# DeltaNet key blocks: decay rows from one 512-column product of diagonals, norms from the diagonals of the key products, one beta scaling per head, both directions of the block inverse in one pass

## The chip, the cores and the metric

One core of a Trainium2 chip. The metric is device time in microseconds (us) of one execution. The engines are TensorE (PE), VectorE (DVE), ScalarE (ACT) and GpSimd (POOL); SyncE (SP) and POOL issue the transfers (DMA). In the profile PEld is TensorE's weight load, which overlaps PE.

## What the kernel computes

A two-layer trunk over 256 context tokens and 256 latent tokens of width 1024. Every layer is half-step SwiGLU, token mixer, half-step SwiGLU; the first mixer is a recurrent scan (RG-LRU), the second is a gated DeltaNet with 8 heads of width 128, in both directions, in chunks of 64 tokens. Only the DeltaNet matters here. For each head and chunk, cut from the reference:

```
k = l2norm(k);  g_cum = cumsum(g)
decay = exp(where(incl, g_cum[:, None] - g_cum[None, :], -inf))
a_mat = where(strict, (k * beta) @ k.T * decay, 0) + eye(64)
sol = triangular_solve(a_mat, concat([v * beta, k * beta * exp(g_cum)]))
qk = (q @ k.T) * decay
```

and then a scan over the chunks with a 128x128 state for each head and direction. There are 4 context and 4 latent chunks, so 8 in each direction.

## The kernel before, in words

Everything is held feature-major: a product has 128 features on the partitions and the tokens as columns. A weight tile is split into a high and a low part, and each 128x128 block of a projection is three products (lines 297 to 299, tile `f` in this stage). The stage `deltanet` (line 953) runs 32 projection tiles of 128 output features, in the order of `SEQ`: 8 of keys, 8 of queries (latent tokens only, 256 columns), then values (512 columns) and output gates (latent only) interleaved. Four key tiles go first, with the stage's norm; the loop at the end of `deltanet` runs the other 28. `project` calls `tick` after every second block of eight, which advances three groups of generators: the decays, the heads' own work (convolution of four taps, one on ACT at line 783 and three on DVE at line 787, then SiLU), and, from the tenth tile on, `keys`.

`keys` starts `k_rest` for one head every four ticks, up to three heads in step, then computes the norms, then runs `solve`, and when the projections of the values are through, `merge`. What stands on each engine in which order is not written out in this stage: the framework's planner orders every engine's instructions from the program order and its own costs. (In the other stages the order of some or all engines is the program's.)

`k_rest` (line 1065) does for one head:

1. ACT squares the keys (lines 1068 and 1048), 512 columns in two instructions.
2. TensorE builds `gr`, 128x512, the cumulated gates of each chunk as rows: for each of two directions and four chunk pairs one 64x64 transpose of a broadcast column (line 1076) and one 64x64 product with the identity (line 1077). A product in full 32-bit floats is two instructions on TensorE, a transpose is one: 24 in all.
3. TensorE forms the sums of the squares with a vector of ones (lines 1080 and 1083, 12 instructions), then the eight 64x64 products of keys with keys, `kk` (line 1087, 16 instructions).
4. DVE subtracts the column gates from `gr` into `e` (line 1091), ACT applies Relu and Exp (lines 1097 and 1098): `e` holds the decay factors. DVE adds the epsilon to the sums of squares (1094), takes the reciprocal (1100) and scales beta by it into `bp` (1102).
5. DVE takes the latent quarter of `e` into `QK` (1108) and multiplies `e` by `kk` (1110).
6. `e` is scaled by `bp` and laid out for the inverse: four 32-row diagonal blocks into `Bc` (line 1118, one on DVE, three on POOL), and four off-diagonal blocks into `MO` (line 1123, all on DVE). Each of the eight instructions does the scaling and the placing at once.

`solve` (line 1210) inverts the 32x32 blocks of all heads by 31 steps of elimination. A step is four DVE instructions: the outer product into `tm` for each direction (line 1223) and the subtraction for each direction (line 1227). Four 128x1024 transposes end it (lines 1230 and 1231). `merge` joins the 32-blocks to 64-blocks with small products on TensorE, and `scan` (line 1358) runs the chunks.

The value and gate weights were split in an earlier stage and kept in DRAM; POOL issues their loads (line 205) into a ring of eight tiles. A POOL load waits until TensorE has read the tile that it replaces. Working tiles of 128x512 come from a pool with five buffers (`phase(5)`).

Of the kernel before, what the change touches and what calls it, by code (L numbers as in the profile page):

```python
# [59 lines left out]
for _name, _w in (("U1", 128), ("L1", 128), ("U1s", 128), ("L1s", 128), ("U1f", 128), ("L1f", 128),  # L60
                  ("CH0", 1), ("CH1", 1), ("cap", 128), ("sel32", 32)):
    MSK[_name] = (_n, _n + _w)
    _n += _w
# [31 lines left out]
def trunk(ctx, tc, io):  # L95
# [853 lines left out]
    def deltanet(norm, next_norm, sp, hp, pools, done):  # L949
# [21 lines left out]
        KQ, QK, VN, Z, KT = ({} for _ in range(5))  # L971
# [5 lines left out]
        def sv(p):  # L977
            return pools[1].tile([128, 32, 32], F32, name=nm(p), tag="sv", bufs=3)
# [10 lines left out]
        def decays(w):  # L989
# [35 lines left out]
            DVE.tensor_copy(gc, q[:, 0:64])  # L1025
            ACT.activation(gt.rearrange("p c x -> p (c x)"), q[:, 192:320], AF.Exp)
# [38 lines left out]
        def k_rest(hd):  # L1065
            kq = KQ[hd]
            sq = slot("sq")
            ACT.activation(sq[:, 0:256], kq[:, 0:256], AF.Square)
            squares(sq[:, 256:512], kq, slice(0, 4, 3))
            yield from pause(PACE["k_lag"])  # L1070
            gr = bank("gr")
            for dr in range(2):
                for j in range(4):
                    o = slice(dr * 256 + j * 64, dr * 256 + j * 64 + 64)
                    c = dr * 32 + j * 8 + hd
                    PE.transpose(gr[LO, o], gc[LO, c:c + 1].to_broadcast([64, 64]), ident[LO, LO])
                    PE.matmul(gr[HI, o], gc[HI, c:c + 1].to_broadcast([64, 64]), ident[HI, HI], start=True, stop=True)
            kk = bank("kk")
            for j in range(2):
                PE.matmul(kk[:, 256 + j:257 + j], sq[:, j * 128:j * 128 + 128], ones, start=True, stop=True)  # L1080
            for i in range(4, 8):
                j = slot_of(i)
                PE.matmul(kk[ROWS[i % 2], 256 + j:257 + j], sq[:, i * 64:i * 64 + 64], ones, start=True, stop=True)
# [9 lines left out]
            rs = small("rs", 4)  # L1093
            DVE.tensor_scalar(rs, kk[:, 256:260], EPS, None, OP.add)
            ACT.copy(ss[:, :, hd], kk[:, 256:260])
            if True:
                ACT.activation(e, e, AF.Relu, scale=-1.0)
            ACT.activation(e, e, AF.Exp, scale=-1.0)
            yield
# [13 lines left out]
            yield  # L1113
            for b in range(4):
                r = slice(32 * b, 32 * b + 32)
                x = slice(32 * (b % 2), 32 * (b % 2) + 32)
                out = Bc[r].rearrange("p d i (s h) -> p d s h i", h=8)[:, :, :, hd]
                (DVE if b < PACE["block_split"] else POOL).tensor_tensor(
                    out, e4[r, :, :, x], dsh(bp)[r, :, :, hd:hd + 1].to_broadcast([32, 2, 4, 32]), OP.mult)
            for dr in range(2):  # L1120
                for c in range(2):
                    r = slice(64 * c + 32 * dr, 64 * c + 32 * dr + 32)
                    (DVE if dr < PACE["mo"] else POOL).tensor_tensor(MO[dr][r, hd::8, :], e4[r, dr, :, 32 * (1 - dr):32 * (1 - dr) + 32],
                                       dsh(bp)[r, dr, :, hd:hd + 1].to_broadcast([32, 4, 32]), OP.mult)
# [85 lines left out]
        def solve():  # L1210
            N, XI = [sv("N") for _ in range(2)], [Bc[:, dr] for dr in range(2)]
# [6 lines left out]
            for j in range(31):  # L1218
                n, m = j + 1, 31 - j
                tm = [pools[1].tile([128, 256], F32, name=nm("tm"), tag="tm", bufs=2)[:, :m * n]  # L1220
                      .rearrange("p (i c) -> p i c", c=n) for _ in range(2)]
                for dr in range(2):
                    DVE.tensor_tensor(tm[dr], N[dr][:, j + 1:, j:j + 1].to_broadcast([128, m, n]),
# [533 lines left out]
```

## Time and profile before

| | us |
|---|---|
| median of 3 runs | 1897.73 |
| lowest, highest | 1894.87, 1900.56 |
| the profiled execution | 1894.58 |
| its span | 1892.8 |
| PE busy in the span | 1827.7 (97%) |
| DVE busy in the span | 1316.6 (70%) |
| ACT busy in the span | 803.3 (42%) |
| POOL busy in the span | 89.5 (5%) |

The span is cut into 40 slices of 47.3 us on the profile's page. "PEclk" is the clock that TensorE was granted, as a share of the full 2.4 GHz; its other level is one half, 1.2 GHz. A busy PE is not PE at its peak: matmuls are pipelined, and a stretch of small products looks as busy as one of large ones.

### The profile page before, as it was taken

What the parts mean: (1) busy time and instruction counts of PE and PEld (TensorE: products, weight loads), DVE (VectorE), ACT (ScalarE), POOL (GpSimd) and SP (SyncE); (2) the same over time, 40 slices, a digit from 0 to 9 for tenths busy, and PEclk for the clock granted to TensorE, in tenths of its full rate; (3) what the DMA queues carried; (4) which work ended last, traced back from release to release, by engine and by line L of the source; (5) the groups of instructions that cost most, each with busy time, mean ns of one, the idle gap of its engine ahead of it and who ended that gap; (6) DMA issues with size and microseconds to landing.
All of it is one profiled execution on the core that took longest, in us unless ns stands there. A gap on an engine that the chain in (4) does not pass through costs nothing.

```text
span 1892.8 us, 29201 instructions
## 1 busy us (share of the span) xinstructions
PE 1827.7 (97%) x11078; PEld 1585.6 (84%) x11078; DVE 1316.6 (70%) x2772; ACT 803.3 (42%) x1651; POOL 89.5 (5%) x130
## 2 busy tenths in 40 slices
PE   5999999999999999999999999999999989889997
PEld 3788888898779888888898888888988886789997
DVE  8867766787888768667466555546756976975555
ACT  5522132247874432333333322323654333845453
POOL 4100000000000000000000000000012230100000
PEclk9999999999999999999999999999978989989999
DMA  8344654542323766566417765743232550035553
GB/s 338 134 158 164 222 175 154 171 159 79 100 82 131 243 236 210 193 226 239 133 56 245 231 213 191 240 146 115 72 101 90 174 157 1 2 122 176 191 178 104
DMA packets 98061, 300.54 MB, mean 159 GB/s; under 512 B 10880, under 2 KB 20352, under 8 KB 97792
## 3 DMA queue, kind: packets, MB, share of 16 engines
q1 hardware_dynamic: 92160, 277.69, 43.6%
q0 software_dynamic: 5760, 20.97, 3.6%
q8 instruction: 87, 1.43, 0.3%
q14 instruction: 54, 0.44, 0.1%
HBM read 276.61 MB, written 22.02 MB: 158 GB/s over the span
## 4 chain that ended last, share of the span: by engine, by line
PE 86%; DVE 6%; issue 4%; ACT 3%; DMA 1%; POOL 0%; SPq 0%; POOLq 0%; DVEq 0%; ACTq 0%
PE gu L298 14%; PE gu L299 14%; PE gu L297 14%; PE fo L297 4%; PE fo L299 4%; PE fo L298 4%; PE tl L297 4%; PE tl L298 4%; PE tl L299 4%; PE f L297 2%; PE f L298 2%; PE f L299 2%; PE p L1416 1%; PE p L1405 1%; DVE hl L501 1%
## 5 line engine op out<-in xcount | busy, mean ns | idle before, releaser
L161 ACT CAST wp<-wr 128x512 fp32r<-128x512 f32 (+1 forms) x689 | 382.8, 607 | 293.8 <-DMA wr<-in_ffn_out_dram 69.3
L162 DVE TENSOR_TENSOR wp<-wr,wp 128x512 fp32r<-128x512 f32 (+1 forms) x689 | 432.7, 674 | 99.7 <-ACT wp L161 95.8
L298 PE MATMUL gu<-hl,wp 128*128 128x512 f32 (+1 forms) x1312 | 479.7, 366 | 9.2 <-DVE hl L501 9.2
L297 PE MATMUL gu<-hh,wp 128*128 128x512 f32 (+1 forms) x1312 | 479.3, 365 | 0.1
L299 PE MATMUL gu<-hh,wp 128*128 128x512 f32 (+1 forms) x1312 | 478.8, 365 | 0.0
L298 PEld LDWEIGHTS gu<-hl,wp 128*128 128x128 f32 x1312 | 248.9, 190 | 50.2 <-DVE hl L501 11.3
L403 DVE SCALAR_TENSOR_TENSOR junk<-ar,cb 128x1024 bf16<-128x1024 f32 x224 | 273.7, 1222 | 22.5 <-DMA ar<-in_w_adaT_dram 18.5
L297 PEld LDWEIGHTS gu<-hh,wp 128*128 128x128 f32 x1312 | 248.9, 190 | 40.4 <-ACT hh L499 0.6
L299 PEld LDWEIGHTS gu<-hh,wp 128*128 128x128 f32 x1312 | 249.1, 190 | 38.8
L653 ACT ACTIVATE sg<-gu 128x512 f32<-128x512 f32 (+1 forms) x88 | 47.8, 543 | 373.0 <-PE gu L299 362.9
L655 DVE TENSOR_TENSOR hf<-sg,gu 128x512 f32<-128x512 f32 (+1 forms) x88 | 54.5, 619 | 184.9 <-PE gu L299 131.2
L297 PE MATMUL tl<-hidh,wp 128*128 128x256 f32 (+1 forms) x418 | 139.7, 334 | 0.0
L298 PE MATMUL tl<-hidl,wp 128*128 128x256 f32 (+1 forms) x418 | 139.3, 333 | 0.0
L299 PE MATMUL tl<-hidh,wp 128*128 128x256 f32 (+1 forms) x418 | 139.2, 333 | 0.0
L297 PE MATMUL fo<-hidh,wp 128*128 128x512 f32 (+1 forms) x352 | 127.6, 362 | 0.0
L298 PE MATMUL fo<-hidl,wp 128*128 128x512 f32 (+1 forms) x352 | 127.6, 362 | 0.0
L299 PE MATMUL fo<-hidh,wp 128*128 128x512 f32 (+1 forms) x352 | 127.6, 362 | 0.0
L297 PE MATMUL f<-H,wp 128*128 128x256 f32 x320 | 98.0, 306 | 1.4 <-ACT sq L1048 1.1
L299 PE MATMUL f<-H,wp 128*128 128x256 f32 x320 | 96.3, 301 | 0.0
L298 PE MATMUL f<-H,wp 128*128 128x256 f32 x320 | 96.2, 301 | 0.0
L298 PEld LDWEIGHTS tl<-hidl,wp 128*128 128x128 f32 x418 | 79.4, 190 | 7.9
L297 PEld LDWEIGHTS tl<-hidh,wp 128*128 128x128 f32 x418 | 79.4, 190 | 7.8
(327 smaller groups left out, 2891.6 us busy)
## 6 DMA issues: line engine op xcount, KB each, us to landing
wr<-in_ffn_in_dram SPq DMA_DIRECT2D x172, 512.0 KB, 4.6
ar<-in_w_adaT_dram SPq DMA_DIRECT2D x128, 512.0 KB, 3.6
wr<-in_ffn_out_dram SPq DMA_DIRECT2D x64, 512.0 KB, 4.9
kp<-wp SPq DMA_DIRECT2D x80, 256.0 KB, 7.2
wp<-kp POOLq DMA_DIRECT2D x40, 512.0 KB, 4.9
wr<-in_dn_in_dram SPq DMA_DIRECT2D x32, 512.0 KB, 3.8
wr<-in_ffn_out_dram SPq DMA_DIRECT2D x64, 192.0 KB, 3.6
wr<-in_lru_in_dram SPq DMA_DIRECT2D x16, 512.0 KB, 4.3
```

Of the source, the lines that this page charges most:

```text
L161: ACT.copy(dst.hi, src)
L162: DVE.tensor_tensor(dst.lo, src, dst.hi.bitcast(F32), OP.subtract)
L297: PE.matmul(out, w.hi, x.hi, start=start, stop=False)
L298: PE.matmul(out, w.hi, x.lo, start=False, stop=False)
L299: PE.matmul(out, w.lo, x.hi, start=False, stop=stop)
L403: DVE.scalar_tensor_tensor(junk, raw, 1.0, cb[:, v], OP.mult, OP.mult, accum_out=m[:, t % 8, v:v + 1])
L501: DVE.scalar_tensor_tensor(lo, t, sh, hi.bitcast(F32), OP.add, OP.subtract)
L653: ACT.activation(sg[:, cols], P[0][:, cols], AF.Silu)
L655: DVE.tensor_tensor(hf[:, cols], sg[:, cols], P[1][:, cols], OP.mult)
L1405: PE.matmul(p2[:, 0:128], Yp[a][:, j * 8 + hd, :], rr, start=True, stop=True)
L1416: PE.matmul(p3[dr][:, 0:128], KT[hd][r2[dr], j * 128:j * 128 + 128], vs[r2[dr]], start=True, stop=True)
```

## The change

- Decay rows. `spread` is new: POOL multiplies an identity mask (`eye`, 64 columns, the same in both halves of the partitions) by the broadcast gate columns of a head into `GD`, 128x512: eight diagonals. `gr` is then one product of a 128x128 block mask of ones (`blk`) with `GD`, 512 columns, in full 32-bit floats. The transposes and the identity products go. Head 0's `GD` is made when the decays are known, each other head's when the head before it starts `k_rest`.
- Norms. The squares on ACT and their 12 TensorE instructions go. DVE multiplies the first 256 columns of `kk` by `eye` and sums each 64 columns (`tensor_reduce`); the result goes to `ss`, which ACT copied before.
- Scaling. DVE multiplies all of `e` by `bp` in one 128x512 instruction. The four `Bc` blocks are then plain copies on POOL (`tensor_scalar` by 1.0 plus 0.0), the four `MO` blocks plain copies on ACT. `k_rest` has one more yield.
- Inverse. The two directions' `N` and `tm` lie in one tile each, and a step is two DVE instructions of twice the size.
- Room: 7 instead of 5 working tiles, 1 instead of 3 buffers of `sv` (the two `N` are one tile of their own), 192 more mask columns, and the buffer for the descriptors of POOL's transfers is set to 8192 bytes for each partition (16384 where nothing is given).

```diff
-            return pools[1].tile([128, 32, 32], F32, name=nm(p), tag="sv", bufs=3)
+            return pools[1].tile([128, 32, 32], F32, name=nm(p), tag="sv", bufs=1)
...
             DVE.tensor_copy(gc, q[:, 0:64])
+            spread(0)
...
         def k_rest(hd):
             kq = KQ[hd]
-            sq = slot("sq")
-            ACT.activation(sq[:, 0:256], kq[:, 0:256], AF.Square)
-            squares(sq[:, 256:512], kq, slice(0, 4, 3))
+            if hd < 7:
+                spread(hd + 1)
             yield from pause(PACE["k_lag"])
+
             gr = bank("gr")
-            for dr in range(2):
-                for j in range(4):
-                    o = slice(dr * 256 + j * 64, dr * 256 + j * 64 + 64)
-                    c = dr * 32 + j * 8 + hd
-                    PE.transpose(gr[LO, o], gc[LO, c:c + 1].to_broadcast([64, 64]), ident[LO, LO])
-                    PE.matmul(gr[HI, o], gc[HI, c:c + 1].to_broadcast([64, 64]), ident[HI, HI], start=True, stop=True)
+            PE.matmul(gr, K_["blk"], GD.pop(hd), start=True, stop=True)
             kk = bank("kk")
-            for j in range(2):
-                PE.matmul(kk[:, 256 + j:257 + j], sq[:, j * 128:j * 128 + 128], ones, start=True, stop=True)
-            for i in range(4, 8):
-                j = slot_of(i)
-                PE.matmul(kk[ROWS[i % 2], 256 + j:257 + j], sq[:, i * 64:i * 64 + 64], ones, start=True, stop=True)
...
-            rs = small("rs", 4)
-            DVE.tensor_scalar(rs, kk[:, 256:260], EPS, None, OP.add)
-            ACT.copy(ss[:, :, hd], kk[:, 256:260])
-            if True:
-                ACT.activation(e, e, AF.Relu, scale=-1.0)
+            ACT.activation(e, e, AF.Relu, scale=-1.0)
             ACT.activation(e, e, AF.Exp, scale=-1.0)
+
+            dg, rs = slot("dg"), small("rs", 4)
+            dv = dg[:, 0:256].rearrange("p (s x) -> p s x", s=4)
+            DVE.tensor_tensor(dv, kk[:, 0:256].rearrange("p (s x) -> p s x", s=4), eye[:, 0].to_broadcast([128, 4, 64]), OP.mult)
+            DVE.tensor_reduce(ss[:, :, hd], dv, mybir.AxisListType.X, OP.add)
+            DVE.tensor_scalar(rs, ss[:, :, hd], EPS, None, OP.add)
...
+            DVE.tensor_tensor(e4, e4, dsh(bp)[:, :, :, hd:hd + 1].to_broadcast([128, 2, 4, 64]), OP.mult)
+            yield
             for b in range(4):
...
-                (DVE if b < PACE["block_split"] else POOL).tensor_tensor(
-                    out, e4[r, :, :, x], dsh(bp)[r, :, :, hd:hd + 1].to_broadcast([32, 2, 4, 32]), OP.mult)
+                POOL.tensor_scalar(out, e4[r, :, :, x], 1.0, 0.0, OP.mult, OP.add)
             for dr in range(2):
                 for c in range(2):
                     r = slice(64 * c + 32 * dr, 64 * c + 32 * dr + 32)
-                    (DVE if dr < PACE["mo"] else POOL).tensor_tensor(MO[dr][r, hd::8, :], e4[r, dr, :, 32 * (1 - dr):32 * (1 - dr) + 32],
-                                       dsh(bp)[r, dr, :, hd:hd + 1].to_broadcast([32, 4, 32]), OP.mult)
+                    ACT.copy(MO[dr][r, hd::8, :], e4[r, dr, :, 32 * (1 - dr):32 * (1 - dr) + 32])
+
+        def spread(hd):
+            GD[hd] = slot("gd")
+            POOL.tensor_tensor(GD[hd].rearrange("p (d s x) -> p d s x", d=2, s=4), eye.to_broadcast([128, 2, 4, 64]),
+                               dsh(gc)[:, :, :, hd:hd + 1].to_broadcast([128, 2, 4, 64]), OP.mult)
...
-                tm = [pools[1].tile([128, 256], F32, name=nm("tm"), tag="tm", bufs=2)[:, :m * n]
-                      .rearrange("p (i c) -> p i c", c=n) for _ in range(2)]
-                for dr in range(2):
-                    DVE.tensor_tensor(tm[dr], N[dr][:, j + 1:, j:j + 1].to_broadcast([128, m, n]),
-                                      XI[dr][:, j:j + 1, :n].to_broadcast([128, m, n]), OP.mult)
-                for dr in range(2):
-                    x = XI[dr][:, j + 1:, :n]
-                    DVE.tensor_tensor(x, x, tm[dr], OP.subtract)
+                tm = pools[1].tile([128, 512], F32, name=nm("tm"), tag="tm", bufs=1)[:, :2 * m * n]
+                tm = tm.rearrange("p (d i c) -> p d i c", d=2, c=n)
+                DVE.tensor_tensor(tm, Nb[:, :, j + 1:, j:j + 1].to_broadcast([128, 2, m, n]),
+                                  Bc[:, :, j:j + 1, :n].to_broadcast([128, 2, m, n]), OP.mult)
+                x = Bc[:, :, j + 1:, :n]
+                DVE.tensor_tensor(x, x, tm, OP.subtract)
...
-    with tc.tile_pool(name="dns", bufs=1, reuse_waits="tile") as dns, phase(5):
+    with tc.tile_pool(name="dns", bufs=1, reuse_waits="tile") as dns, phase(7):
...
-    nc = bacc.Bacc("TRN2", target_bir_lowering=False, num_devices=1)
+    nc = bacc.Bacc("TRN2", target_bir_lowering=False, num_devices=1, dynamic_dma_scratch_size=8192)
```

## Rows read from the trace of the kernel before

**Rows 1.** Busy us by stretch: length, engines (instructions), clock, DMA share, GB/s.

```profile
1383.00:1472.00 89.00, 87.86 (x719) 75.76 (x720) 51.81 (x134) 39.56 (x86) 23.16 (x36) 0.79 0.31 97
1472.00:1539.00 67.00, 65.08 (x668) 63.90 (x667) 64.72 (x179) 22.03 (x64) 20.44 (x34) 0.97 0.65 196
```

**Rows 2.** The same of tile `gr` alone: PE, PEld, DVE, clock, DMA.

```profile
1383.00:1472.00 89.00, 28.71 (x192) 19.08 (x192) 5.53 (x8) 0.79 0.31 97
```

**Rows 3.** The same of tile `kk` alone: PE, PEld, DVE, ACT, clock, DMA.

```profile
1383.00:1472.00 89.00, 15.91 (x224) 15.00 (x224) 6.55 (x16) 1.25 (x8) 0.79 0.31 97
```

**Rows 4.** The same of the projections' tile `f` alone, columns as in Rows 3.

```profile
1383.00:1472.00 89.00, 43.54 (x241) 39.78 (x240) 11.21 (x22) 3.52 (x7) 0.79 0.31 97
1472.00:1539.00 67.00, 60.32 (x466) 58.03 (x466) 15.56 (x21) 7.38 (x14) 0.97 0.65 196
```

**Rows 5.** Busy time in three short stretches, all engines, columns as in Rows 1.

```profile
1386.40:1393.20 6.80, 6.80 (x50) 6.20 (x48) 3.52 (x10) 2.50 (x7) 0.53 (x1) 0.50 0.44 135
...
1472.00:1481.90 9.90, 8.17 (x110) 7.09 (x107) 9.43 (x24) 2.33 (x9) 3.34 (x6) 1.00 0.21 65
1482.00:1485.30 3.30, 3.21 (x15) 3.24 (x16) 3.19 (x8) 1.06 (x4) 0.00 (x0) 0.50 0.39 123
```

**Rows 6.** The chain, one head's sums and key products: start us, us, what.

```profile
1396.23 0.54 PE kk L1080 x4
...
1397.28 0.95 PE kk L1087 x16
```

**Rows 7.** Timeline of TensorE in the scan: 32-bit float products, 128 columns.

```profile
1568.54 0.44 PE L1388 MATMUL p<-S,kq 128*64 128x128 f32 x4
1568.91 0.57 PE L1416 MATMUL p<-vs,kt 64*128 64x128 f32 x4
```

**Rows 8.** DVE by line and shape, 1383 to 1538: count, busy us, mean ns, idle before.

```profile
L1123 DVE TENSOR_TENSOR MO<-e,bp 32x128 f32<-32x128 f32 x32 | 12.2, 381 | 0.3
...
L1166 DVE TENSOR_TENSOR qk<-qk,tq 64x256 f32<-64x256 f32 x16 | 6.7, 418 | 0.4
...
L1110 DVE TENSOR_TENSOR e<-e,kk 128x512 f32<-128x512 f32 x8 | 5.4, 679 | 0.0
L1118 DVE TENSOR_TENSOR Bc<-e,bp 32x256 f32<-32x256 f32 x8 | 5.2, 644 | 0.0
...
L1094 DVE TENSOR_SCALAR rs<-kk 128x4 f32<-128x4 f32 x8 | 1.3, 160 | 7.7 <-PE kk L1087 7.6
```

**Rows 9.** ACT and POOL by line and shape; the last one from the kernel's start.

```profile
L1098 ACT ACT_TABLE_LOAD x4 | 5.1, 1283 | 0.1
L1098 ACT ACTIVATE e<-e 128x512 f32<-128x512 f32 x8 | 5.0, 629 | 0.1
L1118 POOL TENSOR_TENSOR Bc<-e,bp 32x256 f32<-32x256 f32 x24 | 16.5, 686 | 26.7 <-DVE e L1110 15.2 <-DVE rs L1094 5.7 <-ACT kq L1143 2.9
L1534 POOL TENSOR_TENSOR ar<-ar,cb 128x512 f32<-128x512 f32 x16 | 24.3, 1540 | 29.3 <-DVE junk L1532 24.8 <-ACT hh L499 2.4 <-DMA ar<-in_w_adaT_dram 2.1
```

**Rows 10.** Timeline: the four `MO` instructions beside POOL, and later without it.

```profile
1421.08 2.26 POOL L1118 TENSOR_TENSOR Bc<-e,bp 32x256 f32<-32x256 f32 x3 [5.71 <-DVE rs L1094]
1421.42 2.35 DVE L1123 TENSOR_TENSOR MO<-e,bp 32x128 f32<-32x128 f32 x4
...
1431.99 1.17 DVE L1123 TENSOR_TENSOR MO<-e,bp 32x128 f32<-32x128 f32 x4
```

**Rows 11.** Timeline of DVE: a large and a small step of the inverse.

```profile
1508.06 0.76 DVE L1223 TENSOR_TENSOR tm<-N,Bc 128x256 f32<-128x256 f32 x2
1508.73 0.76 DVE L1227 TENSOR_TENSOR Bc<-Bc,tm 128x256 f32<-128x256 f32 x2
...
1527.47 0.34 DVE L1223 TENSOR_TENSOR tm<-N,Bc 128x60 f32<-128x60 f32 x2
1527.73 0.34 DVE L1227 TENSOR_TENSOR Bc<-Bc,tm 128x60 f32<-128x60 f32 x2
```

**Rows 12.** DMA issues of POOL: count, size of one, median us to landing.

```profile
wp<-kp POOLq DMA_DIRECT2D x40, 512.0 KB, 4.9
```

More of the change, by code (lines that the diff above doesn't have):

```diff
@@ L60 @@
 for _name, _w in (("U1", 128), ("L1", 128), ("U1s", 128), ("L1s", 128), ("U1f", 128), ("L1f", 128),
-                  ("CH0", 1), ("CH1", 1), ("cap", 128), ("sel32", 32)):
+                  ("CH0", 1), ("CH1", 1), ("cap", 128), ("sel32", 32), ("blk", 128), ("eye", 64)):
     MSK[_name] = (_n, _n + _w)
@@ L970, in deltanet @@
         ss, ssq, rinv = one("ss", [128, 4, 8]), one("ssq", [128, 2, 8]), one("rinv", [128, 4, 8])
-        KQ, QK, VN, Z, KT = ({} for _ in range(5))
+        KQ, QK, VN, Z, KT, GD = ({} for _ in range(6))
+        eye = K_["eye"][:, None, None, :]
         one("pad", [128, 16])
@@ L1210, in solve @@
         def solve():
-            N, XI = [sv("N") for _ in range(2)], [Bc[:, dr] for dr in range(2)]
+            Nb = pools[1].tile([128, 2, 32, 32], F32, name="N")
+            N, XI = ([t[:, dr] for dr in range(2)] for t in (Nb, Bc))
             for dr in range(2):
@@ L1724, in layout @@
          "cap": np.concatenate([p[:, None] % 64 <= i[None, :], p[:, None] % 64 >= i[None, :]], axis=1)}
+    m["blk"] = same
+    m["eye"] = p[:, None] % 64 == i[None, :]
     m["sel32"] = p[:, None] % 32 == np.arange(32)[None, :]
```

## The prediction

> **What bounds the kernel now.** Read the busy time by stretch first, because the whole span's shares hide the stage that changes. From 1383 us, where the gates are known, to 1472 us, where the inverse begins, lie the key blocks; from 1472 to 1539 us the inverse and the last projections [rows 1]. In the first, the key stretch, TensorE is busy 87.9 of 89.0 us, while DVE has 51.8, ACT 39.6 and POOL 23.2: only TensorE has no room. In the second DVE is busy 64.7 and TensorE 65.1 of 67.0 us: both are full. So in the key stretch a microsecond off TensorE may shorten the time until the next engine is full, and in the other DVE has to shrink for anything to be gained.
>
> Then read what TensorE's 89 us are, by tile. `gr` takes 28.7 [rows 2], `kk` 15.9 [rows 3], the projections 43.5 for 241 products [rows 4]; that is 88.2. In the inverse's stretch 466 products of the same kind take 60.3 us, 0.129 each, so 241 would be 31.2. The missing 12.3 us are the clock: granted 0.79 in the key stretch against 0.97 [rows 1]. The short stretches show the cause's place: from 1386.4 to 1393.2 us, behind a head's burst of `gr` and `kk`, the clock stands at 0.50 (1.2 of 2.4 GHz) although TensorE never rests [rows 5]. The burst costs twice, by itself and by the slower projections behind it.
>
> **TensorE, part by part.** Removed: `gr`, 28.7 us. Removed: the sums of squares. In one head they run from 1396.23 to 1397.28 us, 1.05 us, before the 0.95 us of key products that stay [rows 6]; eight heads 8.4 us. Given back: up to 12.3 us of clock. Added: eight products of 512 columns in 32-bit floats. The trace has none; two such products of 128 columns (four instructions) take 0.37 us from start to start [rows 7], so one of 512 is 4 x 0.185 = 0.74 us and eight 5.9. The ends: 0.26 us if it ran like two projection products [rows 4], 1.5 at half the clock, so 2 to 12 for eight. Sum: 28.7 + 8.4 + 12.3 - 5.9 = 43.5 us off TensorE; 45.5 of 89 remain. That is what the change frees, not what it gains.
>
> **DVE in the key stretch.** Removed: 32 `MO` instructions, 12.2 us, and 8 of `Bc`, 5.2 [rows 8]. Added for each head: the scaling of `e`, the shape of line 1110, 0.68; the masked diagonal, 256 columns with one operand in PSUM, like line 1166, 0.42; the sum over 64 columns, which no row shows: between the smallest instruction, 0.16, and one of 512 columns, 0.68; I take 0.42, as it reads 256. That is 1.52, 12.2 for eight (10.1 to 14.2). The second adding of epsilon stays as it is. POOL slows DVE: the four `MO` took 2.35 us beside 2.26 of POOL and 1.17 without it, 0.52 us lost for one of POOL [rows 10]. POOL loses 16.5 us of `Bc` and gets eight spreads of 1.54 (12.3) [rows 9] and 32 copies, for which half to all of its 0.69 is possible; I take 0.4, since one input is missing, 12.8. POOL is up 8.6 us (6.8 to 17.8), and with half of it beside DVE instructions that feel it, DVE is up 2.3 (0 to 9). DVE: 51.8 - 17.4 + 12.2 + 2.3 = 48.9 us.
>
> The Trainium skill, SBUF — State Buffer, "Who interferes with whom", says that a DVE instruction with two SBUF inputs and a POOL instruction that reads SBUF shut each other out for their whole length. By that the row should show more than the half that it does; with all of 8.6 us lost DVE would stand at 55 and the forecast below some 8 us higher. The row decides.
>
> **ACT and POOL.** ACT loses two squarings a head and the copy of `ss`, and gets 32 copies of 32x128. Its 512-column instruction takes 0.63 [rows 9], so a copy lies between 0.16 and 0.63; 0.3 makes 9.6 us against some 8 removed (16 squarings of half that width, at 0.4 between half and all of 0.63, and eight small copies). ACT stays near 41 us. What is new is that ACT now waits for DVE's scaling; behind it in ACT's queue stand the next queries' convolution and SiLU, which DVE waits for. POOL's waiting instructions hold back its weight loads (line 205). It stands near 32 of 89 us, and the loads wait for TensorE's reading now too. I cost both at nothing because neither engine is full; if that cover is gone, the second rival shows the price. The halved descriptor buffer is costed at nothing: 40 loads of 4.9 us [rows 12] need 196 us if none overlaps another, against the 156 us of the two stretches, so at worst it adds some 40. Two more working tiles can only take waits away; the larger mask is read long after it lands. Both at nothing.
>
> **What the key stretch becomes.** TensorE needs 45.5 us, DVE 48.9, ACT 41. None may be full all the time: a head's work goes from POOL to TensorE, DVE, ACT, DVE and on to POOL and ACT, with up to three heads in step. DVE reaches 58% while it waits for TensorE (51.8 of 89) and 97% in the inverse's stretch, where work always lies ready [rows 1]. I take the middle, 77.5%: 48.9 / 0.775 = 63.1 us, 25.9 less than now.
>
> **The inverse.** Two instructions of 256 columns follow each other in 0.67 us, two of 60 in 0.26 [rows 11]: 0.335 and 0.13 each, so 1.05 ns a column and 0.067 us fixed. Joining 124 instructions to 62 saves 62 x 0.067 = 4.2 us. The ends: if the wider view costs more for each column, as line 1118's scattered 256 columns (0.64 us) do against line 1166's (0.42) [rows 8], 54% on 21,824 columns x 1.05 ns, it would lose 12 us less 4.2, some 8. I take 4.2, because the strides within a direction stay. DVE is full there, so this counts; TensorE is full too, but 63.1 - 45.5 us of room in the key stretch lets projections move ahead.
>
> **Sum.** 25.9 + 4.2 = 30.1 us. The profiled execution took 1894.58 us, 1.8 over its span, and 3.15 under the median; 1894.6 - 30.1 = 1864.5, and 1867.6 on the median's scale. I forecast 1868 us, with an own range of 1860 to 1876.
>
> **Rivals.**
>
> 1. *TensorE's whole gain arrives.* DVE works at 97% in the key stretch too: 48.9 / 0.97 = 50.4, 38.6 off, with 4.2 it is 42.8: 1855 us. For it: 7.7 us of DVE's idle time there ended at `kk` before line 1094 alone [rows 8]. Against it: the chain through two ACT instructions and table loads of 1.28 us stays [rows 9].
>
> 2. *The hand-offs, not the burst, held DVE.* It stays at 58%: 48.9 / 0.58 = 84.3, 4.7 off, with 4.2 it is 8.9: 1889 us. For it: the head gets longer by a scaling and two steps for the norm before anything leaves. Against: TensorE is at 99% now, so DVE could not have been faster.
>
> 3. *The clock stays low.* From 1472 to 1481.9 us, with no `gr`, TensorE worked 8.2 of 9.9 us at 1.00, and the next 3.3 us were granted 0.50 [rows 5]: waits and small products can bring the half clock as well. With the projections at 43.5, the new products doubled to 11.8 and 7.5 of key products and 0.8 of the rest, TensorE needs 63.6 us, 25.4 off; it then has no room to run ahead, and the inverse gives nothing: 1872 us. The Trainium skill, TensorE: Matmul & The Clock Gate, "A second HAM failure mode: psum-queue depth-cycling", says that short idles between groups of matmuls make the clock swing between its levels; by that the new waits of TensorE for DVE bring back what the burst's removal gave, and the first rival is out. The trace has the one case just read.
>
> 4. *Slower: one head at a time.* The new `GD` of a head stands in POOL's queue behind the head before's copies, which wait for DVE's scaling, and behind weight loads that wait for TensorE. If that closes the ring, a head costs its whole chain: spread 1.54, product 0.74, key products 0.95, subtraction 0.68, Relu and Exp 1.26 with a table load 1.28, `QK` 0.84, two passes over `e` 1.36, four copies 1.6, and a query tile in the same queues (three DVE instructions at 0.51, one of ACT at 0.5 [rows 4], a table load back 1.28): 13.6 us. A head now takes 89 / 8 = 11.1, so 8 x 2.5 = 20 more, less 4.2: 1913 us. It decides from 11.7 us a head. Against it: the spread is asked for a head ahead.
>
> **Chances.** Forecast 0.42, first rival 0.20, second 0.15, third 0.14, fourth 0.07, the descriptor buffer 0.02. A measurement of this kernel tells 0.3% from no change, 5.7 us: so slower begins at 1903 us and faster ends at 1892. Slower is the fourth and most of the buffer's chance, 0.08; within 0.3% is the second gone a little worse and what is left of the buffer's, 0.05; faster is the rest, 0.87. The range 1850 to 1890 leaves out the fourth, the buffer, the upper part of the second and a little under the first.
>
> **What would show it.** `gr` on TensorE at 16 instructions and near 6 us; the clock in the key stretch above 0.95 (third rival: under 0.85); from the gates to the first transpose of the inverse 63 us (50: first rival, 84: second, over 100: fourth); DVE at 49 us there; the 62 steps of the inverse near 27 us. The forecast is wrong if the clock recovers and the key stretch still is above 75 us, or if DVE's steps of the inverse take more than before.

## The result, and the profile after the change

The changed kernel takes 1856.32 us (median of four runs, 1852.03 to 1857.31); the kernel before, run beside it, takes 1898.60 (four runs, 1894.87 to 1900.56). The ratio is 0.9775, with a 95% interval of 0.9753 to 0.9797: faster by 42 us. That lies in the range of 1850 to 1890 us, 12 us below the forecast and outside its own range; it is the first rival's number.

The profiled execution took 1857.31 us with a span of 1855.5, 37.3 us less span than before. To place these, cut both traces at the same events: the copy of the gates (`gc`), the first transpose of the inverse, its last one, the first copy of `KT`. The rows are busy time by stretch in the changed kernel, key stretch first, then inverse (columns as in [rows 1]):

```profile
1381.20:1435.90 54.70, 50.25 (x450) 42.96 (x450) 53.94 (x131) 48.96 (x103) 38.74 (x52) 0.95 0.52 164
1435.90:1499.90 64.00, 64.00 (x588) 62.77 (x586) 61.49 (x110) 23.14 (x69) 19.43 (x32) 0.99 0.66 201
```

Between the same events the kernel before takes 89.8 and 64.4 us. The key stretch gives 35.1 of the 37.3 us, the inverse 0.4; the merge behind it gives 2.4, the stretch ahead of the gates 1.2, and the rest is 1.8 longer. The granted clock in the key stretch is 0.95, where it was 0.79 [rows 1], and VectorE (DVE) is busy for 53.94 of 54.7 us, 98.6%, where it was at 58%. By tile of TensorE in this key stretch, `gr`, then `kk`, then `f` (columns as in [rows 2] and [rows 3]):

```profile
1381.20:1435.90 54.70, 8.31 (x16) 2.42 (x16) 5.45 (x8) 0.95 0.52 164
1381.20:1435.90 54.70, 5.48 (x128) 4.41 (x128) 8.43 (x16) 0.95 0.52 164
1381.20:1435.90 54.70, 39.31 (x274) 35.24 (x274) 13.10 (x27) 4.27 (x9) 0.95 0.52 164
```

`gr` fell from 28.71 to 8.31 us [rows 2], `kk` from 15.91 to 5.48 [rows 3], and 274 projection products now cost less than 241 did [rows 4]. The groups of DVE and of POOL in that stretch (count, busy us, mean ns of one, idle us before them) answer to [rows 8] and [rows 9]:

```profile
L162 DVE TENSOR_TENSOR wp<-wr,wp 128x512 fp32r<-128x512 f32 x8 | 8.2, 1030 | 0.0
L1102 DVE TENSOR_TENSOR qk<-e,msk 64x256 f32<-64x256 f32 x16 | 8.1, 507 | 0.2
...
L1108 DVE TENSOR_TENSOR e<-e,bp 128x512 f32<-128x512 f32 x8 | 5.5, 682 | 0.0
L1083 DVE TENSOR_TENSOR e<-gr,gc 128x512 f32<-128x512 f32 x8 | 5.5, 682 | 0.1
...
L1090 DVE TENSOR_TENSOR dg<-kk,msk 128x256 f32<-128x256 f32 x8 | 3.3, 417 | 0.0
L1091 DVE TENSOR_REDUCE ss<-dg 128x4 f32<-128x256 f32 x8 | 3.3, 415 | 0.0
```

```profile
L1114 POOL TENSOR_SCALAR Bc<-e 32x256 f32<-32x256 f32 x32 | 22.5, 704 | 5.5 <-DVE rst L316 1.1 <-DVE rs L1092 1.1 <-DVE e L1108 0.9
L1122 POOL TENSOR_TENSOR gd<-msk,gc 128x512 f32<-128x512 f32 x8 | 9.3, 1166 | 62.7 <-DVE gc L1026 59.5 <-DVE ss L1091 2.9
```

The idle column of DVE is the point: next to nothing stands in it, where 7.7 us of waiting for `kk` stood before one line alone [rows 8]. More stood before line 1091 of the kernel before, in its stretch between the same events:

```profile
L787 DVE SCALAR_TENSOR_TENSOR u<-f,cst,u 128x255 f32<-128x255 f32 (+3 forms) x23 | 11.7, 508 | 8.9 <-ACT u L783 8.8
...
L1091 DVE TENSOR_TENSOR e<-gr,gc 128x512 f32<-128x512 f32 x8 | 5.5, 692 | 18.2 <-PE gr L1077 10.3 <-PE kk L1083 7.9
```

### The profile page after: what moved, and what is told of

The parts are those of the page before. It is cut to its first block, busy times and chain, and to the rows that moved or that the text cites. A ratio compares the mean times of both kernels' runs of the same rounds, so it can differ in the third digit from the quotient of the medians.

```text
span 1855.5 us, 28613 instructions
## 1 busy us (share of the span) xinstructions
PE 1788.4 (96%) x10806; PEld 1551.2 (84%) x10806; DVE 1315.2 (71%) x2694; ACT 809.7 (44%) x1661; POOL 105.2 (6%) x146
## 4 chain that ended last, share of the span: by engine, by line
PE 84%; DVE 8%; issue 4%; ACT 3%; DMA 2%; SPq 0%; POOL 0%; POOLq 0%; ACTq 0%; DVEq 0%
PE gu L298 14%; PE gu L297 14%; PE gu L299 14%; PE fo L298 4%; PE fo L297 4%; PE fo L299 4%; PE tl L297 4%; PE tl L299 3%; PE tl L298 3%; PE f L297 2%; PE f L298 2%; PE f L299 2%; PE p L1414 1%; DVE wp L162 1%; PE p L1403 1%
## 5 line engine op out<-in xcount | busy, mean ns | idle before, releaser
L297 PE MATMUL f<-H,wp 128*128 128x256 f32 x320 | 94.2, 294 | 0.0
L299 PE MATMUL f<-H,wp 128*128 128x256 f32 x320 | 92.4, 289 | 1.0 <-DVE wp L162 1.0
L298 PE MATMUL f<-H,wp 128*128 128x256 f32 x320 | 92.1, 288 | 0.0
```

The lines of the kernel that those rows point to most:

```text
L297: PE.matmul(out, w.hi, x.hi, start=start, stop=False)
L298: PE.matmul(out, w.hi, x.lo, start=False, stop=False)
L299: PE.matmul(out, w.lo, x.hi, start=False, stop=stop)
```

## The experiments

Each time is a median over four runs (ten for "no rows" and "split burst"), each ratio is to the kernel before on the same chip with its 95% interval; "key" is the key stretch, cut as above.

### Which part of the change pays

**Rows only.** The kernel before with the changed kernel's decay rows (`spread`, the product with `blk`, and the room for it), the rest as before.

```diff
...
-                    PE.transpose(gr[LO, o], gc[LO, c:c + 1].to_broadcast([64, 64]), ident[LO, LO])
-                    PE.matmul(gr[HI, o], gc[HI, c:c + 1].to_broadcast([64, 64]), ident[HI, HI], start=True, stop=True)
+            PE.matmul(gr, K_["blk"], GD.pop(hd), start=True, stop=True)
...
```

> The kernel before with the decay rows alone changed (one product of diagonals, GD by POOL), and the room of the kernel after (7 working tiles, 8192 bytes for descriptors, the masks); norms, scaling and inverse as before. Theory: the burst on TensorE was the key stretch's bound, so nearly all of the gain comes back with it: TensorE 28.7 us and 12 us of clock less, 8 us more for the new products, about 57 us for the stretch; 1858 to 1868 us. Rival (the hand-offs and DVE's own work paced the stretch, and the norms and the scaling brought the time): over 1880 us, DVE's share in the stretch under 0.75.

1868.19 us, ratio 0.9851 (0.9817 to 0.9885): 30 us of the 42, just past the edge of what was expected. The key stretch missed it by more: 66.3 us where 57 were expected, at clock 0.93, and DVE is already the full engine (62.74 us):

```profile
1380.80:1447.10 66.30, 57.55 (x556) 50.55 (x555) 62.74 (x143) 46.14 (x96) 33.54 (x44) 0.93 0.44 136
```

**No rows.** The changed kernel with the old transposes and products for its decay rows (the diff above the other way round).

> The kernel after with the decay rows as before (64x64 transposes and identity products), all else after. Theory: TensorE is the bound again, 28.7 us back for 8.3 and half clock behind each burst: key stretch about 80 to 88 us instead of 54.7, 1882 to 1892 us. Rival (norms and scaling brought the time): under 1872 us.

1889.02 us (median of ten), ratio 0.9951 (0.9923 to 0.998). Key 84.8 us, TensorE busy for 83.15 of them, clock 0.82:

```profile
1381.00:1465.80 84.80, 83.15 (x650) 70.46 (x650) 51.48 (x134) 49.33 (x104) 28.56 (x44) 0.82 0.35 106
```

Without the new rows the other three edits, with the room, are worth some 9 us (4 to 15 by the interval).

**Scaling back.** The changed kernel with the four `Bc` and four `MO` instructions of before, each scaling its own block, in place of `L1108` and the copies.

```diff
...
-            DVE.tensor_tensor(e4, e4, dsh(bp)[:, :, :, hd:hd + 1].to_broadcast([128, 2, 4, 64]), OP.mult)
...
-                    ACT.copy(MO[dr][r, hd::8, :], e4[r, dr, :, 32 * (1 - dr):32 * (1 - dr) + 32])
+                    (DVE if dr < PACE["mo"] else POOL).tensor_tensor(MO[dr][r, hd::8, :], e4[r, dr, :, 32 * (1 - dr):32 * (1 - dr) + 32],
+                                       dsh(bp)[r, dr, :, hd:hd + 1].to_broadcast([32, 4, 32]), OP.mult)
```

> The kernel after with scaling and placing at once as before, eight instructions on DVE and POOL, none on ACT. Theory (DVE paces the stretch): DVE loses 5.5 us of scaling and gets 5.2 of Bc and 9 to 12 of MO, POOL loses some 6: DVE up 5 to 9 us, ACT down 9.4; stretch 59 to 63 us, 1860 to 1865 us. Rival (ACT at 90% or the hand-off to ACT paces it): the stretch gets shorter, 1850 us or less.

1870.58 us, ratio 0.9872 (0.9845 to 0.9898): 14 us more than the changed kernel (18 by the two ratios), more than was expected. DVE fills the longer key stretch, 67.07 of 68.2 us, 13 us more than in the changed kernel where 5 to 9 were expected, and its `MO` instructions take 508 ns where they took 381 [rows 8]. Stretch and group of this kernel:

```profile
1380.60:1448.80 68.20, 55.60 (x454) 47.80 (x453) 67.07 (x159) 40.66 (x72) 32.33 (x44) 0.87 0.42 132
```

```profile
L1117 DVE TENSOR_TENSOR MO<-e,bp 32x128 f32<-32x128 f32 x32 | 16.2, 508 | 0.3
```

The clock is 0.87 in this stretch, though no transpose is left in `gr`. It dips where TensorE has waited for DVE, as in these two windows of all engines, one after the other:

```profile
1409.00:1413.00 4.00, 0.93 (x18) 0.66 (x16) 3.96 (x7) 3.41 (x6) 3.47 (x5) 1.00 0.85 280
1413.00:1417.00 4.00, 2.83 (x13) 2.83 (x14) 3.91 (x13) 0.46 (x2) 0.02 (x1) 0.58 0.15 22
```

**Norms back.** The changed kernel with the squares on ACT and their products with ones.

```diff
...
-            DVE.tensor_reduce(ss[:, :, hd], dv, mybir.AxisListType.X, OP.add)
...
+                PE.matmul(kk[:, 256 + j:257 + j], sq[:, j * 128:j * 128 + 128], ones, start=True, stop=True)
...
```

> The kernel after with the norms as before: squares on ACT, 12 small TensorE instructions a head, no masked diagonal and no sum on DVE. Theory (in the key stretch of the kernel after DVE is full at 98.6%, ACT at 90%, TensorE at 92%): DVE loses 6.6 us, TensorE gains some 8 and ACT 6.5 and both are over-full at 58 and 55 us, so the stretch is 57 to 61 us instead of 54.7: 1858 to 1863 us. Rival (only DVE paces it): 48 to 50 us for the stretch, 1850 us. Rival (the norms brought the time): over 1868 us.

1857.61 us, ratio 0.9799 (0.9767 to 0.9831): not told from the changed kernel, and just under the theory's range, clear of both rivals. The row gives a reason: 6 us leave DVE, and TensorE is full instead, in 54.2 us where 57 to 61 were expected.

```profile
1382.30:1436.50 54.20, 54.20 (x580) 48.78 (x580) 47.78 (x114) 49.60 (x129) 39.00 (x52) 1.00 0.51 159
```

**Inverse back.** The changed kernel with the four DVE instructions a step of before.

```diff
...
-                DVE.tensor_tensor(x, x, tm, OP.subtract)
...
+                for dr in range(2):
+                    x = XI[dr][:, j + 1:, :n]
+                    DVE.tensor_tensor(x, x, tm[dr], OP.subtract)
...
```

> The kernel after with the inverse as before (four instructions a step, the two directions apart, two buffers of tm). Theory from the trace after: a joined instruction depends on the one just before it and starts 0.03 us after its end (0.725 us from start to start at 512 columns), where two apart of 256 overlapped (0.67 us for the two), so joining gains nothing: within 3 us of the kernel after, 1853 to 1859 us, rather faster than slower. Rival, the prediction's working: 62 fixed costs of 0.067 us come back, 4.2 us slower, 1860 us.

1855.35 us, ratio 0.9784 (0.975 to 0.9818); the inverse's stretch is 62.2 us against 64.0. Joining the directions gains nothing that can be told. The timeline of DVE in the changed kernel (start us, us, instruction) shows the large steps, which answer to [rows 11]:

```profile
1469.79 0.69 DVE L1225 TENSOR_TENSOR Bc<-Bc,tm 128x510 f32<-128x510 f32 x1
1470.51 0.69 DVE L1222 TENSOR_TENSOR tm<-N,Bc 128x512 f32<-128x512 f32 x1
1471.24 0.69 DVE L1225 TENSOR_TENSOR Bc<-Bc,tm 128x512 f32<-128x512 f32 x1
```

A joined instruction starts 0.72 to 0.73 us after the one before, two separate ones took 0.67 together [rows 11]. There the second of a pair starts before the first has ended (two in a record of 0.76 us, the next record 0.67 after its start); here each instruction needs the one just before it and starts 0.03 us after its end. Over the whole inverse, counting each instruction up to the next one's start and leaving out waits for ACT, the steps hold DVE for 31.4 us in 124 instructions before and for 32.7 in 62 after; some 1.5 of the 32.7 are the gaps behind an instruction's end.

### What made the old decay rows dear

**Split burst.** The kernel before with the 24 instructions of a head's `gr` in four groups, projections let in between.

```diff
                 for j in range(4):
+                    if j % 2 == 0 and dr + j:
+                        yield
                     o = slice(dr * 256 + j * 64, dr * 256 + j * 64 + 64)
```

> The kernel before, its 24 instructions of a head's decay rows split by yields into four groups that stand between projection products; the same work on every engine. Theory: it is the unbroken burst of small products that brings the half clock; with projections between them the clock in the key stretch rises from 0.79 to above 0.95 and the 12.3 us read for the clock come off, less some for the later hand-offs: 1886 to 1891 us. Rival: small products anywhere lower the clock, it stays near 0.8, and the time is 1895 to 1902 us.

1906.58 us, ratio 1.0057 (1.0036 to 1.0079): slower, where the theory expected a gain. In the key stretch of 101.6 us the clock is 0.75, lower than before, and `gr` costs 34.53 us, more than before; the row is that of `gr` alone:

```profile
1386.70:1488.30 101.60, 34.53 (x192) 21.59 (x192) 5.52 (x8) 0.75 0.31 96
```

The mean hides two levels; all engines, in four pieces of that stretch:

```profile
1386.70:1414.00 27.30, 27.30 (x246) 21.93 (x246) 15.47 (x38) 14.52 (x32) 4.90 (x8) 1.00 0.39 128
...
1417.60:1446.00 28.40, 28.40 (x162) 23.49 (x162) 13.00 (x37) 9.23 (x20) 6.03 (x10) 0.50 0.31 93
1450.50:1457.20 6.70, 6.70 (x48) 5.14 (x46) 4.40 (x10) 3.79 (x7) 3.29 (x5) 1.00 0.26 78
1457.30:1470.00 12.70, 12.70 (x73) 9.92 (x72) 5.92 (x12) 4.71 (x7) 2.02 (x3) 0.50 0.14 43
```

In the first piece three heads' groups stand apart, and the clock holds at 1.00. In the fourth, fifth and sixth heads three of the four groups run in one piece all the same, the first time from 1414.62 to 1417.60 us, and the clock is at 0.50. The seventh head's groups stand apart again (1450.58 to 1456.70), yet the clock falls behind them. So a long unbroken burst is not needed for the fall; that its length plays a part this run does not rule out.

**No transposes.** The kernel before with one line changed: the upper half's transposes written as the products that the lower half uses.

```diff
-                    PE.transpose(gr[LO, o], gc[LO, c:c + 1].to_broadcast([64, 64]), ident[LO, LO])
+                    PE.matmul(gr[LO, o], gc[LO, c:c + 1].to_broadcast([64, 64]), ident[LO, LO], start=True, stop=True)
```

> The kernel before with its eight transposes a head as products with the identity (two instructions each, the same result); nothing else. Question: what lowers the clock. If transposes are what the clock does not count, it stays at 1.0 in the key stretch (0.79 before), some 12 us come off and some 6 are added for the second instruction: 1890 to 1895 us. If any run of such small products lowers it, the clock stays below 0.85 and the time is 1899 to 1908 us.

1866.58 us, ratio 0.9848 (0.9821 to 0.9875). One line brings as much as "rows only", without the room, and neither theory foresaw that. The key stretch:

```profile
1383.50:1442.00 58.50, 53.08 (x746) 50.00 (x746) 53.33 (x131) 44.08 (x85) 22.03 (x34) 0.95 0.48 151
```

TensorE's timeline in the kernel before (it goes on in this way for all eight pairs), then with the line changed:

```profile
1383.02 0.24 PE L1076 MATMUL gr<-ident,gc 64*64 64x64 f32 x1
1383.19 0.32 PE L1077 MATMUL gr<-ident,gc 64*64 64x64 f32 x2
1383.44 0.24 PE L1076 MATMUL gr<-ident,gc 64*64 64x64 f32 x1
1383.61 0.32 PE L1077 MATMUL gr<-ident,gc 64*64 64x64 f32 x2
```

```profile
1384.29 0.22 PE L1076 MATMUL gr<-ident,gc 64*64 64x64 f32 x1
1384.30 0.22 PE L1077 MATMUL gr<-ident,gc 64*64 64x64 f32 x1
1384.35 0.22 PE L1076 MATMUL gr<-ident,gc 64*64 64x64 f32 x1
1384.36 0.22 PE L1077 MATMUL gr<-ident,gc 64*64 64x64 f32 x1
```

A transpose and its product take 0.425 us from start to start, and a head's eight pairs 3.39 (1383.02 to the first `kk` at 1386.41). As products, the two halves start 0.01 us apart and the next two follow after 0.06: 1.08 us for a head (1384.19 to 1385.27), though there are 32 instructions in place of 24. Two readings were left: the transposes are dear by themselves, or the change from one kind to the other is.

**Grouped.** The kernel before with the same 8 transposes and 8 products for each head, all transposes first.

```diff
-            for dr in range(2):
-                for j in range(4):
...
+            for half in (LO, HI):
+                for dr in range(2):
+                    for j in range(4):
...
+                        if half == LO:
+                            PE.transpose(gr[LO, o], gc[LO, c:c + 1].to_broadcast([64, 64]), ident[LO, LO])
+                        else:
+                            PE.matmul(gr[HI, o], gc[HI, c:c + 1].to_broadcast([64, 64]), ident[HI, HI], start=True, stop=True)
```

> The kernel before, with the same eight transposes and eight products of a head's decay rows, but all eight transposes first and then all eight products. Theory (it is the alternation that costs, each change between a transpose and a product letting the engine run empty): a head's rows take 1.0 to 1.6 us of TensorE in place of 3.39, the clock of the key stretch is over 0.9, and the time is 1866 to 1874. Rival (each transpose costs its 0.24 to 0.43 us whatever stands beside it): 2.4 to 3.4 us a head, 1885 to 1900.

1865.39 us, ratio 0.9833 (0.9803 to 0.9863): some 32 us by the order of the same instructions. Since products on the two halves alternate without a price ("no transposes"), it is the change to and fro between the kinds that costs. Timeline of one head's `gr` and what follows it, then the key stretch by all engines, then by `gr`, `kk` and `f`:

```profile
1384.35 0.63 PE L1078 MATMUL gr<-ident,gc 64*64 64x64 f32 x8
1384.91 1.14 PE L1080 MATMUL gr<-ident,gc 64*64 64x64 f32 x16
1385.98 0.49 PE L1083 MATMUL kk<-ones,sq 128*128 128x1 f32 x3
```

```profile
1383.70:1443.50 59.80, 58.66 (x727) 54.61 (x726) 53.84 (x137) 40.26 (x87) 23.80 (x36) 1.00 0.46 147
...
1383.70:1443.50 59.80, 13.60 (x192) 11.79 (x192) 5.49 (x8) 1.00 0.46 147
1383.70:1443.50 59.80, 11.22 (x224) 10.45 (x224) 6.46 (x16) 1.27 (x8) 1.00 0.46 147
1383.70:1443.50 59.80, 33.97 (x247) 30.31 (x246) 11.70 (x23) 3.52 (x7) 1.00 0.46 147
```

A head takes 1.63 us (1384.35 to 1385.98). The key stretch falls by 30.0 us, and TensorE's tiles account for it: `gr` 28.71 to 13.60 (15.1), `kk` 15.91 to 11.22 (4.7), and the 247 projection products 10.2, from 44.20 in the same stretch of before. So half of the price was paid in `gr` itself and half by what stood behind it, through the clock (some of `gr`'s half is clock as well). Compare a burst and what follows it before, where the second window stands in [rows 5] with 50 TensorE instructions in 6.8 us at 0.50, with the same two windows of "grouped" behind it:

```profile
1383.00:1386.40 3.40, 3.40 (x25) 2.32 (x24) 0.96 (x2) 1.31 (x7) 0.73 (x1) 1.00 0.57 200
```

```profile
1384.30:1386.10 1.80, 1.80 (x26) 1.60 (x26) 1.01 (x4) 1.34 (x8) 0.73 (x1) 1.00 0.22 61
1386.10:1393.00 6.90, 6.90 (x100) 6.44 (x101) 5.76 (x15) 4.29 (x9) 0.98 (x2) 1.00 0.88 288
```

In 6.9 us 100 instructions go through at 1.00, right behind 1.8 us of grouped `gr`. Between these two kernels the order alone decides whether the granted clock falls to its lower level (1.2 GHz) behind `gr`. The order also halves the time that `gr` takes, so whether the clock falls by the changes between the kinds or by the longer run of small instructions stays open. The Trainium skill, TensorE: Matmul & The Clock Gate, "Part 4: PE-mode transpose", says that the upper clock is not engaged for transposes, because they do not count as the engine's being busy in the same way. Here it stays at 1.00 through a key stretch with all 64 transposes in it, so transposes as such are not what lowers it. A head loses 1.76 us (3.39 less 1.63) by 14 changes more, 0.13 us a change; why a change costs that (whether the array must run empty, for instance) no run shows.

### What bounds the changed kernel now

**Product twice.** The changed kernel with each `blk` product issued a second time.

```diff
-            PE.matmul(gr, K_["blk"], GD.pop(hd), start=True, stop=True)
+            gd = GD.pop(hd)
+            PE.matmul(gr, K_["blk"], gd, start=True, stop=True)
+            PE.matmul(gr, K_["blk"], gd, start=True, stop=True)
```

> The changed kernel with each head's 512-column product issued twice, so TensorE does 8 products more (two passes each of 0.26 us at the upper clock, some 4.2 us in all). Theory (VectorE, busy for 98.6% of the key stretch, bounds it, and TensorE at 50.3 of 54.7 us has 4.4 us to spare): 1856 to 1859. Rival (TensorE still bounds it, by waits that its busy share hides): 1860 to 1865.

1855.97 us, ratio 0.9783 (0.9751 to 0.9815): no price that can be told, though the interval reaches into the rival's range. TensorE is full in the key stretch with it (6.1 us more, where 4.2 were expected) and DVE still at 95%:

```profile
1379.10:1436.00 56.90, 56.31 (x493) 45.05 (x492) 53.92 (x133) 51.50 (x107) 38.74 (x52) 1.00 0.50 158
```

The stretch itself is 2.2 us longer than in the changed kernel, about as long as TensorE now needs. It ends at the same time, because the gates were ready 2.1 us earlier in this execution (1379.1 against 1381.2 us), ahead of the first added product. So by the profile TensorE bounds the key stretch here.

**Identity rows.** The changed kernel with its decay rows from 16 identity products, as in "no transposes": `spread` and the `blk` product go.

```diff
...
-            PE.matmul(gr, K_["blk"], GD.pop(hd), start=True, stop=True)
...
+                    PE.matmul(gr[LO, o], gc[LO, c:c + 1].to_broadcast([64, 64]), ident[LO, LO], start=True, stop=True)
+                    PE.matmul(gr[HI, o], gc[HI, c:c + 1].to_broadcast([64, 64]), ident[HI, HI], start=True, stop=True)
```

> The changed kernel, with its decay rows taken from 16 products of broadcast gate columns with the identity (no transposes among them, no spread on POOL, no 512-column product). Theory (the change gained by taking the alternation of transposes and products off TensorE, and VectorE now bounds the key stretch): such a head's rows cost TensorE 0.94 us, as in the kernel without transposes, about the 1.04 us of the 512-column product with its two passes, and POOL loses 9.3 us beside VectorE's 53.9, so the key stretch is 51 to 54.7 us and the time 1852 to 1857. Rival 1 (the single 512-column product itself is the gain): 128 small products bring back some 10 us on TensorE, 1864 or more. Rival 2 (POOL's work does not slow VectorE): 1856 to 1858.

1853.15 us (1852.06 to 1857.17), ratio 0.9775 (0.9737 to 0.9812), the same ratio as the changed kernel: equal within what can be told, so the 512-column product has no merit of its own that shows. Key 53.6 us. Two DVE groups, then busy time in it (POOL, fifth, is at 29.36 us):

```profile
L1104 DVE TENSOR_TENSOR qk<-e,msk 64x256 f32<-64x256 f32 x16 | 6.9, 432 | 0.3
L162 DVE TENSOR_TENSOR wp<-wr,wp 128x512 fp32r<-128x512 f32 x9 | 6.2, 705 | 0.0
```

```profile
1380.20:1433.80 53.60, 51.59 (x698) 48.67 (x698) 50.59 (x135) 48.45 (x102) 29.36 (x44) 0.97 0.55 168
```

**Identity rows and old norms.** The same, and the norms as in "norms back".

> As the kernel with decay rows from 16 identity products, and in addition the norms from squares on ScalarE and products with ones, as before the change. Theory (with the norms back, VectorE falls to 46 to 48 us and TensorE, 54.2 of 54.2 us with the old norms, is the bound at about 54): 1853 to 1858. Rival (VectorE's own length decides in both, so six microseconds less of it come off): 1848 to 1851.

1863.18 us, ratio 0.9822 (0.9792 to 0.9853): against both theories, some 10 us over "identity rows". DVE has fallen to 46.44 of 63.6 us, TensorE stands at 58.11, and ACT is the full engine at 59.22:

```profile
1380.40:1444.00 63.60, 58.11 (x785) 55.57 (x785) 46.44 (x119) 59.22 (x129) 28.71 (x44) 0.94 0.47 142
```

```profile
L1099 ACT ACT_TABLE_LOAD x7 | 9.0, 1283 | 0.1
L1155 ACT ACT_TABLE_LOAD x6 | 7.7, 1283 | 0.1
```

These are the two lines where ACT changes between Exp and SiLU: 13 table loads in the key stretch, where "norms back", with the same instructions on ACT, has 7. Six loads of 1.283 us are 7.7 us, most of the 9.6 by which ACT is busier than there. That the heads fall into another step and that this makes the time is read from these rows; no run tests it.

**No blocks.** The changed kernel without POOL's `Bc` copies for seven of the eight heads; it computes other numbers for them.

```diff
-                POOL.tensor_scalar(out, e4[r, :, :, x], 1.0, 0.0, OP.mult, OP.add)
+                if hd == 0:
+                    POOL.tensor_scalar(out, e4[r, :, :, x], 1.0, 0.0, OP.mult, OP.add)
...
+        POOL.memset(Bc, 0.0)
```

> The kernel after with POOL's copies into Bc left out for heads 1 to 7 (Bc set to zero once; so the inverse works on other numbers), 28 copies of 0.70 us less on POOL, none of them on DVE's own work. Theory (POOL's copies slow DVE's instructions with two SBUF operands, which took 1.03 us instead of 0.67 at line 162): DVE's busy time in the stretch falls from 53.9 to 48 to 51 us and the stretch with it, 1850 to 1853 us. Rival (POOL costs DVE nothing): 54.7 us for the stretch less at most 1.5 for the last copy, 1855 to 1857 us.

1860.32 us, ratio 0.9818 (0.979 to 0.9847): not faster. The inverse no longer waits for the last blocks and starts at 1421.6 us, amid the key heads, which moves the mark; key and inverse together take 119.3 us against 118.7. The time and the stretches settle nothing about what POOL's copies cost DVE, but one group bears on it (1382.4 to 1421.6 us, where POOL does eight spreads and four copies):

```profile
L162 DVE TENSOR_TENSOR wp<-wr,wp 128x512 fp32r<-128x512 f32 x8 | 8.0, 1005 | 0.0
```

With nearly all copies gone, line 162 stays at 1005 ns (1030 in the changed kernel).

## Why the prediction came out as it did

- *TensorE bounds the key stretch, and `gr` with its clock is what it loses*: right. It needs 50.25 us, 3.9 of them for 27 projection products that moved ahead (39.31 / 274 each), so 46.4 for the old work against 45.5 predicted. A `blk` product costs 1.04 us (8.31 / 8), not 0.74; the norms' instructions and the clock made it up in `kk` (10.4 us in place of 8.4).
- *The burst brings the low clock*: right in its place, incomplete in its reason. The prediction took the burst as a whole for the cause. "Grouped" shows that the order within it decides: 32 of the change's 42 us can be had by reordering one loop. The 12.3 us that the prediction read for the clock in the projections measured 10.2 there.
- *The working share of 77.5% for DVE*: this step failed. It was a middle between two levels, 58% and 97% [rows 1], not a reading. Of DVE's 37 us of idle time before, 26 ended at TensorE (lines 1091 and 1094) and most of the rest at ACT's line 783; the hand-offs to ACT and POOL that the change adds cost nothing that DVE's rows show, and it went to 98.6%: the first rival's 97%. Its length was mis-sized the other way, 53.94 us (about 52.5 without the four convolution instructions that moved ahead) against 48.9, and the two misses partly cancel: 53.94 / 0.986 = 54.7, predicted 63.1.
- *POOL's copies at 0.4 us, and half of its work felt by DVE*: a copy took 0.704, so losing the second input gave nothing [rows 9]; spreads took 1.17, not 1.54. In the key stretch DVE lost 0.356 us on each of 8 at line 162 (1030 ns, 674 before) and 0.026 on each of 16 at line 1102 (507, 481 before in the whole stretch, there line 1108): 3.3 us, where 2.3 was taken. With the spreads gone and the 32 copies kept ("identity rows"), the two lines take 705 and 432 ns. So it is the two-input spread that DVE feels, and much less the copies; "no blocks", with the spreads kept and nearly all copies gone, agrees (1005 ns). In the changed kernel line 162 takes 1.91 us beside a spread (1388.58) and 0.66 beside copies (1409.05). The Trainium skill, SBUF — State Buffer, "Who interferes with whom", counts any GpSimd read of SBUF against a DVE instruction with two SBUF inputs; the copies read SBUF too, and the rows here put most of the loss on the spreads.
- *The 0.42 us taken for reduction and diagonal, the 0.68 for the scaling*: 0.415, 0.417 and 0.682 measured. For the diagonal and the scaling, rows of the same shape and operand place priced them well; the reduction's 0.42 was a guess between two bounds, and came out by luck.
- *The inverse, 4.2 us from joining*: failed; the stretch is 0.4 shorter, the steps hold DVE 1.3 longer (32.7 against 31.4, where 27 was forecast), and "inverse back" finds no difference. Counted so, one of the prediction's own signs of being wrong came: the steps take more than before. The fixed part of an instruction is hidden when an independent one follows; joined, every instruction depends on the last, so the overlap went with the instruction count.
- *ACT and POOL at nothing*: held, but narrowly. ACT takes 48.96 us, 89% of the key stretch, not 41 of 63 (two more table loads are 2.6 us of it); "identity rows and old norms" is a case in which it is the fullest engine and the time is 10 us longer.
- *Rivals*: two (hand-offs) and four (slower) are out, by the idle column of DVE. Three (low clock) is out at 0.95; one dip is left in the key stretch, behind 4 us from 1429 in which TensorE works 1.45. Its mechanism, that waits of TensorE bring the half clock, is not out: where DVE bounds, in "scaling back", the clock dips behind such waits.
- *The first rival's number*: 42.8 us, 42.3 measured, and that is luck in part. It was 38.6 from the key stretch and 4.2 from the inverse; the profiles give 35.1 and 0.4, and the rest came from the merge and the stretch ahead of the gates, which no term covers, and from runs that differ by some us.

By parts: the rows alone give 30 us; taken from the whole, the rows are worth 33, the scaling 14, norms and inverse nothing that can be told. No run takes out the room by itself. What the scaling brings while TensorE still bounds was not run; without the new rows all three other edits bring 9. DVE is the fullest engine of the changed kernel's key stretch, but not by much: six microseconds less of DVE ("norms back") or six more of TensorE ("product twice") leave the time as it is, each time with TensorE full. With TensorE at 92%, DVE at 98.6% and ACT at 89% of the key stretch, the edits here that moved work between them only changed which is full.

## What to carry over

Before replacing a group of small TensorE instructions by something larger, look at their start-to-start times, and try them sorted by kind: the order can be most of the price (32 of 42 us here), and a slow burst is paid again by the work behind it at the lower clock. When the full engine is relieved, take the next engine at nearly its full share unless a row shows it idle for another reason. Joining instructions gained nothing here, where two independent ones already overlapped.

## What was not expected of the hardware

- TensorE: a 64x64 transpose followed by a 64x64 product takes 0.425 us in alternation; eight transposes in a row 0.56 us, 16 product passes in a row 1.07, and products on the two halves of the partitions run beside each other, 0.06 us for one of each.
- The same transposes and products, grouped, leave the granted clock at 1.00; alternated, it fell to 0.50 behind the bursts (mean 0.79), and with the bursts cut up it fell later and stayed down longer (0.75).
- DVE: a chain of dependent 512-column instructions runs at 0.725 us each, a little longer than two independent ones of 256 columns (0.67 for both).
- POOL: a 32x256 copy with one input takes 0.704 us, the product with two inputs took 0.686 [rows 9].
